# One convolution moved to TensorE, a recurrence cut into two joined segments, and five smaller moves in a hybrid S5 / RWKV-7 layer

## The chip, the cores and the metric

One Trainium2 chip, one of its cores. The metric is the device time of one execution of the whole program in microseconds; three runs of the kernel before gave 1879.26, 1881.02 and 1885.11, and the median, 1881.02, is its time. A separate profiled execution gave the trace that is read below.

## The reference, cut to what matters

A layer over 512 latent tokens with 256 context tokens in front, width 1024, all in fp32. The context goes through the first FFN and the mixers only for the states that it leaves.

```
mod = silu(c) @ w_mod + b_mod            # 9 x 1024, for latents and for context
x   = half_ffn(x);  ctx = half_ffn(ctx)  # SwiGLU, 1024 -> 2816 -> 1024
_, states = token_mixers(modulate(ctx), rows=1, zero states)
out, _    = token_mixers(modulate(x), rows=8, states)
x   = half_ffn(x + mod5 * out);  return rmsnorm(x)

token_mixers(h):  proj = h @ w_in        # u (S5), r k v (RWKV), small ranks, two gates
  S5, both directions, 32 groups x 64 complex states:  s[t] = A s[t-1] + B u[t];  y = C s
  r, k, v = 3x3 depthwise convolution of an image of rows x (n / rows)
  RWKV-7, both directions, 8 heads:  S = S w + (S a) b + v k;  y = S r
  merge: GLU of the S5 output, group norm of the RWKV output, projections, gates, w_out
```

## The kernel before, in words

**Dense work.** Every large product is three matmuls in fp32r, from a high and a low part of the weights and of the activations. A weight block of 128x1024 is loaded from SP's queue (`raw`), rounded by ScalarE (`wh`), and its rest (`wl`) is taken by GpSimd or, where that would be late, by VectorE. The blocks stand in one list, `items`: the context's first FFN, the latents' first FFN with the context's `w_in` blocks between, the latents' `w_in` blocks, then GLU, `w_o`, projection, `w_out` and the second FFN. The generator `dense` works them off in this order.

**What sets the order.** A planner (class `Plan`) runs at build time. Each part is a generator that stops at `yield` with what it needs: tiles, named events, or a pair such as `("P", 3000)`, "GpSimd's planned queue is at most 3000 ns ahead". The planner keeps an estimated clock of each engine, one of the port that GpSimd and VectorE share, and one of the DMA queue, and always runs on the stream of best priority that is ready. So the order of instructions on each engine is fixed when the program is built; on the chip each engine only waits in that order.

**Modulation.** `mod_run` (528) multiplies silu(c) with `w_mod`, in 72 loads of 128 x 4 x 256 (512 KB). 40 of them (shifts, scales and gates 0 to 4) stand at the start, 32 (`fill_run`) beside the latents' first mixer stage. In memory a partition's four rows of 256 lie apart, so each load is in pieces of 1 KB.

**S5.** A chunk is 8 tokens. `s5_build` (957) makes, while the context is worked on, the chunk matrices of 16 pairs of groups for each direction: G (input to state, on GpSimd, X tiles), H (state to output, in `outputs`, on VectorE alone, H tiles), and the impulse response, which goes through memory (Kd, KTd, KTe) into Toeplitz form. It posts `s5b` at its end, after

```
        yield [self.KTd]
        for s in range(8):
            nc.sync.dma_start(self.KTe[s], ...)
        self.sch.post("s5b")
```

`ctx_run` (910) waits for `s5b` before it sets up the context's RWKV stage. `s5_in` fills `hs` with the chunks' inputs, `s5_rec` (1749) runs the recurrence over chunks on GpSimd, four operations of 128 x 64 for each chunk (32 for the context, 64 for the latents):

```
            Pg.tensor_mul(t1, self.arr, h[:, c - 1])
            Pg.tensor_mul(t2, self.aii, h[:, c - 1, ::-1])
            Pg.tensor_add(t1, t1, h[:, c])
            Pg.tensor_add(h[:, c], t1, t2)
```

and `s5_out` (1769) waits for it, then loads H and the Toeplitz blocks and makes the outputs, which `s5_post` turns into the GLU's input. While the latents' recurrence runs, all `wl` go to VectorE.

**RWKV.** First stage (`phase_b1`): `conv_evac` copies a `w_in` block of r, k or v into one of two zero-bordered buffers (10 x 66 for the latents) and scales it with the middle tap; `conv` adds the other eight taps on VectorE. `win_mm` doesn't evacuate block n before convolution n - 2 is done. `v_rows` transposes v on PE, `pa` makes the decays, `pn` the normalised keys, and `pb` (1373) the operands `st`: with tiles `nb`, `kt` and four products on GpSimd, four or five on VectorE, for 4 pairs of heads and two directions. `st` has one buffer, written out by DMA. Second stage (`phase_b2`, for the context in `ctx_run`): `rw_solve` inverts 32x32 triangles for four chunks at a time on VectorE, starting from an identity that GpSimd writes with `affine_select`; `rw_pre` and `rw_main` go through the chunks, 4 for the context and 8 for the latents. In the latents' second stage the gates' `w_in` blocks are run between as filler.

## Time and profile before

| | us |
|---|---|
| median of three runs | 1881.02 (1879.26 to 1885.11) |
| the profiled execution | 1882.93 |
| its span | 1881.2 |
| PE busy | 1681.7 (89%) |
| VectorE (DVE) busy | 1008.5 (54%) |
| ScalarE (ACT) busy | 716.1 (38%) |
| GpSimd (POOL) busy | 655.1 (35%) |

The profiled execution lies 1.7 us above its span and 1.9 us above the median. PE is TensorE's matmuls; the granted clock is given as a share of 2.4 GHz, its other level being 1.2 GHz (0.50). All instructions carry the line of one helper, so groups are told apart by tile names: `wl` is the low part of a weight block, `cvv` the convolved v, `H` and `ms`/`X` the S5 matrices, `t`/`hs` the recurrence, `st` the RWKV operands, `T` and `ti` the solve's result, `yg` the GLU's input. A number such as "x63 | 25.9, 412" is a count, the busy us in all, and the mean ns of one.

### The profile page before, as it was taken

What the parts mean: (1) busy time and instruction counts of PE and PEld (TensorE: products, weight loads), DVE (VectorE), ACT (ScalarE), POOL (GpSimd) and SP (SyncE); (2) the same over time, 40 slices, a digit from 0 to 9 for tenths busy, and PEclk for the clock granted to TensorE, in tenths of its full rate; (3) what the DMA queues carried; (4) which work ended last, traced back from release to release, by engine and by line L of the source; (5) the groups of instructions that cost most, each with busy time, mean ns of one, the idle gap of its engine ahead of it and who ended that gap; (6) DMA issues with size and microseconds to landing.
All of it is one profiled execution on the core that took longest, in us unless ns stands there. A gap on an engine that the chain in (4) does not pass through costs nothing. (4 is left out here: it accounts for less than half of the span.)

```text
span 1881.2 us, 33153 instructions
## 1 busy us (share of the span) xinstructions
PE 1681.7 (89%) x13208; PEld 1409.2 (75%) x13208; DVE 1008.5 (54%) x1763; ACT 716.1 (38%) x1200; POOL 655.1 (35%) x799
## 2 busy tenths in 40 slices
PE   6899999899999989768976879969799999999996
PEld 3699997778887877666544657758689988888886
DVE  3376563755558737444788755644357533333335
ACT  3355442445453213434434323434443342222221
POOL 0134231466664313721334526950015321111111
PEclk9999989899999999887988969979899999999998
DMA  9956551335555464424753484637555223233331
GB/s 308 326 179 193 185 157 58 108 104 148 147 162 150 142 195 154 119 94 130 228 182 101 135 252 150 171 108 199 168 200 181 68 79 101 90 99 102 96 96 56
DMA packets 235626, 278.42 MB, mean 148 GB/s; under 512 B 93617, under 2 KB 186801, under 8 KB 234449
## 3 DMA queue, kind: packets, MB, share of 16 engines
q1 hardware_dynamic: 235472, 276.32, 48.3%
q8 instruction: 104, 1.70, 0.4%
q14 instruction: 50, 0.40, 0.1%
HBM read 234.31 MB, written 43.22 MB: 148 GB/s over the span
## 5 line engine op out<-in xcount | busy, mean ns | idle before, releaser
L209 PE MATMUL b<-hx,wh 128*128 128x512 f32 (+1 forms) x2432 | 704.6, 377 | 19.0 <-ACT wh L209 10.6
L209 POOL TENSOR_TENSOR wl<-raw,wh 128x1024 fp32r<-128x1024 f32 x119 | 292.2, 2457 | 805.7 <-ACT wh L209 748.4
L209 PEld LDWEIGHTS b<-hx,wh 128*128 128x128 f32 x2432 | 444.4, 197 | 103.7 <-issue 16.2
L209 PE MATMUL b<-hx,wl 128*128 128x512 f32 (+1 forms) x1216 | 451.4, 371 | 7.5 <-POOL wl L209 6.5
L209 DVE TENSOR_TENSOR wl<-raw,wh 128x1024 fp32r<-128x1024 f32 x154 | 213.2, 1385 | 291.0 <-ACT wh L209 288.7
L209 ACT CAST wh<-raw 128x1024 fp32r<-128x1024 f32 x273 | 283.1, 1046 | 192.8 <-DMA raw<-in_wgu 67.8
L209 PEld LDWEIGHTS b<-hx,wl 128*128 128x128 f32 x1216 | 238.2, 196 | 48.1 <-POOL wl L209 8.8
L209 PE MATMUL b<-ah,wh 128*128 128x512 f32 (+1 forms) x560 | 196.3, 351 | 0.0
L209 PE MATMUL b<-ah,wl 128*128 128x512 f32 (+1 forms) x560 | 194.4, 347 | 0.3 <-POOL wl L209 0.3
L209 PE MATMUL b<-al,wh 128*128 128x512 f32 (+1 forms) x560 | 194.6, 347 | 0.0
L209 PE MATMUL b<-hc,wh 128*128 128x256 f32 x928 | 174.1, 289 | 1.5 <-ACT hc L209 1.2
L209 PEld LDWEIGHTS b<-hc,wh 128*128 128x128 f32 x928 | 146.5, 193 | 12.6 <-issue 10.0
L209 PE MATMUL b<-hc,wl 128*128 128x256 f32 x464 | 132.0, 284 | 0.0
L209 PEld LDWEIGHTS b<-ah,wl 128*128 128x128 f32 x560 | 107.4, 192 | 13.5 <-POOL wl L209 0.5
L209 PEld LDWEIGHTS b<-ah,wh 128*128 128x128 f32 x560 | 107.3, 192 | 12.7 <-issue 0.2
L209 ACT CAST ah<-prod 128x512 fp32r<-128x512 f32 (+1 forms) x68 | 36.6, 538 | 210.6 <-DVE prod L209 210.6
L209 PEld LDWEIGHTS b<-al,wh 128*128 128x128 f32 x560 | 107.3, 192 | 12.5 <-DVE al L209 0.4
L209 ACT ACTIVATE sil<-b 128x512 f32<-128x512 f32 (+1 forms) x68 | 35.0, 515 | 153.6 <-PE b L209 153.5
L209 DVE TENSOR_TENSOR prod<-sil,b 128x512 f32<-128x512 f32 (+1 forms) x68 | 39.6, 582 | 95.2 <-PE b L209 75.7
L209 PEld LDWEIGHTS b<-hc,wl 128*128 128x128 f32 x464 | 89.6, 193 | 0.0
L209 DVE SCALAR_TENSOR_TENSOR x1c<-b,gp,x1c 128x512 f32<-128x512 f32 (+1 forms) x67 | 43.9, 662 | 74.5 <-PE b L209 74.5
L209 PE MATMUL b<-wmod,zs 128*32 128x256 f32 x576 | 55.7, 478 | 23.4 <-DMA wmod<-in_wmod 23.1
(289 smaller groups left out, 2327.4 us busy)
## 6 DMA issues: line engine op xcount, KB each, us to landing
raw<-in_wgu SPq DMA_DIRECT2D x132, 512.0 KB, 3.8
wmod<-in_wmod SPq DMA_DIRECT2D x72, 512.0 KB, 5.5
raw<-in_wdn SPq DMA_DIRECT2D x66, 512.0 KB, 3.7
raw<-in_win SPq DMA_DIRECT2D x49, 512.0 KB, 3.9
gt<-GTd SPq DMA_DIRECT2D x32, 256.0 KB, 4.0
abk<-st SPq DMA_DIRECT2D x8, 1024.0 KB, 5.8
AB<-abk SPq DMA_DIRECT2D x8, 1024.0 KB, 6.9
GTd<-gst SPq DMA_DIRECT2D x16, 256.0 KB, 2.4
```

The source lines that it names most:

```text
L209: r = f(out, *args, **kw)
```

## The change

1. `w_mod` is laid out in memory so that each load of 512 KB has 4 KB in one piece for a partition.
2. In `s5_build`, VectorE also makes the powers 1 to 16 of the chunk's factor, which are stored (`s5P`). `outputs` takes its work from a list that two streams share: VectorE from the front, GpSimd, when it is through with G, from the back. `s5b` is posted before the KTe copies, and these wait for the end of the context's mixers (`rwc`).
3. For the latents, v is convolved on PE: nine matmuls of a diagonal of the tap's weights (made by GpSimd) with the shifted block, in PSUM. r and k stay on VectorE. The buffers have no border any more; each tap works on the part that it reaches. There are three of them, and block n waits for convolution n - 3.
4. In `pb`, the latents' four GpSimd products go to VectorE. In `pa`, one tile is dropped.
5. `rw_solve`'s identity is two fills by VectorE.
6. The latents' recurrence is cut into two halves of 32 chunks that advance side by side, in operations of 128 x 128; then the second half gets the first's last state times the powers, two chunks at a time. It begins after the event `b2`.
7. `s5_out` asks for its first loads before the recurrence has ended.

```diff
-                nc.sync.dma_start(ws[-1], self.a["wmod"][j, :, k:k + 4, u * 256:(u + 1) * 256])
+                nc.sync.dma_start(ws[-1], self.a["wmod"][j, u, k // 4])
...
+        ps = [half("X").rearrange("p a (k r c) -> p (a k) r c", r=2, c=32) for _ in range(2)]
+        V.tensor_copy(ps[0][:, 0], pw[:, 8])
+        for k, n, o in ((1, 1, (0, 1)), (2, 2, (0, 2)), (4, 4, (0, 4)), (8, 8, (1, 0))):
+            f, d = ps[0], ps[o[0]][:, o[1]:o[1] + n]
+            bc = lambda i: f[:, k - 1, i, None, :].to_broadcast([128, n, 32])
+            cmul(d[:, :, 0], d[:, :, 1], bc(0), bc(1), f[:, 0:n, 0], f[:, 0:n, 1], [t[:, :n] for t in m4], V)
+        for i in range(2):
+            nc.sync.dma_start(self.s5P[:, 8 * i:8 * i + 8], ps[i])
...
+        left = list(range(16))
+
+        def outputs(V, e, names, end):
...
+                if left:
+                    n = left.pop(end)
+                    nxt = [n, *load(n, names[0], a["s5C"])]
...
+                    if o:
+                        V.tensor_scalar(Ct[:, 1], Ct[:, 1], -1.0, None, op0=OP.mult)
...
+        self.sch.add(outputs(V, "V", ("hc", "H", "mh"), 0), S5P)
...
+        yield from outputs(Pg, "P", ("hb", "X", "ms"), -1)
+        yield ["s5hV"]
...
-        yield [self.KTd]
+        self.sch.post("s5b")
+        yield ["rwc", self.KTd]
         for s in range(8):
             nc.sync.dma_start(self.KTe[s], self.KTd[:, :, 7 - s:15 - s].rearrange("i g l o -> i g (l o)"))
-        self.sch.post("s5b")
...
+            w = 2 if r.v else q
+            yield [f"conv{r.s}{n - w}"] * (n >= w) + [f"pb{r.s}{n // q - 2}", f"vr{r.s}{n // q - 2}"] * (n >= 2 * q)
...
+        if r.cvq and not (M_R <= m < M_WD and self.cv_name(m) in ONPE):
+            yield from self.conv_mm(r)
...
+    def taps(self, r, ch):
+
+        self.dg = r.q.tile([128, 9, 128], F32, name="dg")
+        self.nc.gpsimd.affine_select(self.dg, self.cw[:, ch, :, None].to_broadcast([128, 9, 128]),
+                                     pattern=[[0, 9], [1, 128]], base=0, channel_multiplier=-1,
+                                     compare_op=OP.is_equal, fill=0.0)
+
+    def conv_mm(self, r):
...
+        pad, dg = r.pads[n % 3], self.dg
+        yield [pad, dg]
+        px = self.dbank()
...
+        for i, t in enumerate((4, 0, 1, 2, 3, 5, 6, 7, 8)):
+            o, i_ = self.reach(t)
+            self.nc.tensor.matmul(o3[o], dg[:, t], i3[i_], start=i == 0, stop=i == 8, skip_group_check=True)
...
+                B = Pg if r.v else V
...
-                Pg.tensor_mul(nb, fw(nkk, d), ic)
-                Pg.tensor_mul(kt, kt, fw(k, d))
+                B.tensor_mul(nb, fw(nkk, d), ic)
...
-        nc.gpsimd.affine_select(Tt, self.ones[:, 0:32][:, :, None].to_broadcast([128, 32, 32]),
...
+        V.memset(Tt, 0.0)
+        V.memset(Tt.rearrange("p a b -> p (a b)")[:, ::33], 1.0)
...
+        yield [f"s5in{r.s}"] + ["b2"] * (n == 2)
...
+            hc, m = h[:, 1:65].rearrange("p (s c) r k -> p s c r k", s=2), 32
...
+        for c in range(1, m):
+            step((t1, t2, hc[:, :, c]), hc[:, :, c - 1], ar, ai)
             yield [("P", RECP)]
+        for c in (32, 48) if n == 2 else ():
+            Pg.tensor_scalar(sw[:, 0], h[:, c, 1], -1.0, None, op0=OP.mult)
+            Pg.tensor_copy(sw[:, 1], h[:, c, 0])
+            for k in range(0, 16, 2):
...
+                Pg.tensor_mul(t1, p[:, :, 0:1].to_broadcast(w), h[:, c:c + 1].to_broadcast(w))
+                Pg.tensor_mul(t2, p[:, :, 1:2].to_broadcast(w), sw[:, None].to_broadcast(w))
+                Pg.tensor_add(t1, t1, t2)
+                Pg.tensor_add(o, o, t1)
+                yield [("P", RECP)]
...
     def s5_out(self):
...
-        yield ["s5recx"]
+        yield ["s5tab"]
...
         nxt, hts = load_t(0), [load(i) for i in range(HB - 2)]
+        yield ["s5recx"]
```

## Rows read from the trace of the kernel before

**Rows 1.** The page: busy us by engine, and PE's busy tenths by slice.
```profile
PE 1681.7 (89%) x13208; PEld 1409.2 (75%) x13208; DVE 1008.5 (54%) x1763; ACT 716.1 (38%) x1200; POOL 655.1 (35%) x799
...
PE   6899999899999989768976879969799999999996
```
**Rows 2.** Busy time by stretch: stretch, length, engines (instructions), granted clock, DMA share, GB/s.
```profile
0.00:97.00 97.00, 73.66 (x585) 47.81 (x585) 34.75 (x87) 32.88 (x66) 11.82 (x19) 1.00 0.96 318
698.00:806.00 108.00, 84.51 (x1197) 69.87 (x1195) 56.90 (x109) 41.58 (x92) 54.61 (x133) 0.88 0.50 143
877.00:1107.00 230.00, 178.81 (x1394) 120.23 (x1395) 167.44 (x227) 94.22 (x155) 89.39 (x74) 0.83 0.55 168
1230.00:1344.00 114.00, 83.65 (x1956) 74.96 (x1956) 44.32 (x92) 43.14 (x91) 19.64 (x53) 0.88 0.53 151
```
**Rows 3.** PE's waits, 0 to 103 us: for what, total, times, longest.
```profile
PE b L209 <- DMA wmod<-in_wmod: 14.2, 14, 5.0
```
**Rows 4.** DMA issues: count, size of one, median us to landing.
```profile
raw<-in_wgu SPq DMA_DIRECT2D x132, 512.0 KB, 3.8
wmod<-in_wmod SPq DMA_DIRECT2D x72, 512.0 KB, 5.5
```
**Rows 5.** PE's waits, 680 to 806 us.
```profile
PE b L209 <- DVE M L209: 5.8, 1, 5.8
```
**Rows 6.** Timeline of VectorE at two points: start, us, operation.
```profile
582.84 0.43 DVE L209 TENSOR_TENSOR H<-mh 128x256 f32<-128x256 f32 x1
...
662.24 0.42 DVE L209 SCALAR_TENSOR_TENSOR H<-mh 128x256 f32<-128x256 f32 x1
```
**Rows 7.** PE's waits, 877 to 1107 us.
```profile
PE b L209 <- DVE cvv L209: 15.5, 3, 8.0
PE b L209 <- DMA wmod<-in_wmod: 7.6, 6, 3.2
...
PE b L209 <- POOL st L209: 5.0, 2, 3.6
```
**Rows 8.** Groups by shape, 877 to 1107 us: VectorE, then PE.
```profile
L209 DVE SCALAR_TENSOR_TENSOR cvv<-pad,cw,cvv 128x512 f32<-128x512 f32 x32 | 29.8, 930 | 0.8
...
L209 DVE TENSOR_TENSOR st<-nb,em 64x512 f32<-64x512 f32 x8 | 10.4, 1304 | 1.2 <-POOL nb L209 1.2
...
L209 DVE TENSOR_TENSOR st<-cvr,ep 128x512 f32<-128x512 f32 x8 | 6.4, 804 | 0.1
...
L209 PE MATMUL b<-vs,flip 128*128 128x512 f32 x8 | 7.2, 1004 | 1.1 <-ACT vs L209 1.1
L209 PE MATMUL b<-ks,rkb 128*128 128x512 f32 x8 | 5.2, 742 | 0.6 <-DVE ks L209 0.6
```
**Rows 9.** Tile ms: GpSimd's G products, ns least/median/most, first and last start.
```profile
L209 POOL TENSOR_TENSOR ms<-pz,hb x64: 636/650/1636, 349.2 to 542.6; 128x256 f32<-128x256 f32 x64
```
**Rows 10.** Timeline of PE round one rkb product.
```profile
1068.02 1.02 PE L209 MATMUL b<-ks,rkb 128*128 128x512 f32 x2
1068.88 0.49 PE L209 MATMUL b<-ident,rb 128*128 128x128 f32 x3
```
**Rows 11.** Groups by shape on GpSimd, 1107 to 1260 us.
```profile
L209 POOL TENSOR_TENSOR t<-t,hs 128x64 f32<-128x64 f32 x63 | 25.9, 412 | 15.2 <-ACT hs L209 15.2
...
L209 POOL TENSOR_TENSOR hs<-t,t 128x64 f32<-128x64 f32 x63 | 23.5, 374 | 4.9
L209 POOL TENSOR_SCALAR_AFFINE_SELECT Tl<-ones 128x1024 f32<-128x1024 f32 x2 | 3.4, 1678 | 12.9 <-DMA ti<-Tl 12.8
```
**Rows 12.** Timeline of GpSimd: the recurrence's last operation.
```profile
1250.03 0.32 POOL L209 TENSOR_TENSOR hs<-t,t 128x64 f32<-128x64 f32 x1
```
**Rows 13.** Tile Tz: PE's Toeplitz products, ns least/median/most, first and last start.
```profile
L209 PE MATMUL b<-U,Tz x128: 222/222/270, 1275.1 to 1332.3; 128*64 128x64 f32 x128
```
**Rows 14.** PE's waits, 1230 to 1345 us.
```profile
PE b L209 <- ACT yg L209: 7.2, 1, 7.2
```
**Rows 15.** Groups by shape, whole span: GpSimd's G products.
```profile
L209 POOL TENSOR_TENSOR ms<-pz,hb 128x256 f32<-128x256 f32 x64 | 51.0, 816 | 3.3 <-DVE pz L209 1.9
```

151 lines of the change are left out of this document (95 added, 56 removed).

## The prediction

> **What bounds the kernel now.** I read the busy shares first, then the 40 slices, then busy time by stretch, then the waits of the stretches in which TensorE (PE) rests, and at the end single instructions. PE is busy for 1681.7 of 1881.2 us, and most slices read 9 [rows 1]; so the long dense stretches are full, and only PE's idle time, its slow clock and work that is added to PE or taken from it can move the end. The low slices are the first, those round 700 to 800 us, those of 880 to 1110 us, and those round 1240 us. In the table by stretch [rows 2] PE lacks 23.3 us in 0 to 97 us (span less busy time), 23.5 in 698 to 806, 51.2 in 877 to 1107 and 30.4 in 1230 to 1344: 128 of its 199 idle us. The edits lie in or just before these four places, so I price each there.
>
> The profiled execution took 1882.9 us (span 1881.2 and 1.7 around it); the median of the three runs is 1.9 lower. I sum against 1882.9 and take 1.9 off at the end.
>
> **Start (wmod in one piece per partition).** 40 of the 72 wmod loads of 512 KB lie before 97 us; the DMA queues are 0.96 busy there at 318 GB/s [rows 2], and PE waits 14.2 us for wmod, 5.0 of it for the very first load [rows 3]. A weight load of the same size, already in 4 KB pieces, lands in 3.8 us against 5.5 [rows 4]. If that ratio held under full load, the 21 MB of wmod (66 us at 318 GB/s) would shrink by 20 us, more than the waits; if HBM is the limit, by nothing. Of the 9.2 us that are not the first wait I take -6; ends 0 and -14. In the Trainium skill, "DMA: Bandwidth & Descriptors" (Why small descriptors are slow) charges a packet some three cycles beside one for each 32 bytes: 35 cycles for 1 KB, and 131 rather than 140 for 4 KB. By that estimate the 66 us shrink by only 4 us, and the sum would be 2 us less good than mine. The other 32 loads feed the fill in 877 to 1107, where PE waits 7.6 us for them [rows 7]: -2, ends 0 and -5.
>
> **Context: H shared by VectorE and GpSimd, and the KTe copies moved.** GpSimd ends its 16 G groups at 544 [rows 9], when VectorE has finished four of its 16 H groups; the other twelve run from 582.8 to 662.7, 6.6 us each [rows 6, 9]. After the change GpSimd goes on at 544 from the far end. One group costs it four products and two differences of the shape of its G products, 0.65 us each [rows 9], and a small negation: some 4.3 us bare, 6 with the waits that VectorE shows. By 583 it has done six, and the last six split between two engines end near 603, not 663. The new power table costs VectorE about 6 us ahead of G (24 small products at 0.2 to 0.4 us), and the eight KTe copies, with the wait for KTd to land, no longer stand before the event s5b: about 7 us by the eight issues and a landing. So the context's mixer starts some 60 us earlier. What that is worth is PE's idle time in 698 to 806: there the context's recurrence runs with the dense FFN used up, and PE waits longest for masks that VectorE makes behind the solve [rows 5]. Dense work is the same in sum; beside it the chain's holes are filled. Of the 23.5 idle us I take -17, since the last context step and the tail behind it still wait for each other; ends 0 and -30 (all of the idle time and 7 us of its 0.88 clock). The KTe issues come back behind the event rwc, on SP ahead of weight loads; their 6 us stood ahead of weight loads before as well, so I set that move to nothing net, the tail's three loaded blocks hiding it; uncovered it costs up to 6 us.
>
> **Convolution of v on PE, and VectorE for GpSimd's products.** VectorE loses the 32 taps of cvv, 29.8 us [rows 8]. It gains four products for each of eight rounds; VectorE's own of that length cost 1304 ns where GpSimd multiplies beside it, and 804 where it mostly doesn't [rows 8]. At 0.75 us that is 24 us for 32; at 1304 it would be 42. Its old products lose their competitor: about 0.5 us on 24 of them, 12 us, and some 5 on the remaining taps. So VectorE sheds some 23 of its 167 busy us in the stretch, and GpSimd 48 (with four diagonals of 128x1152 added, under 2 us each).
> PE gains nine fp32 matmuls for each of four blocks, on average 464 of 512 columns wide. None stands in the trace; the nearest row is the rkb product, 128x128 by 512 fp32: four of them take 5.2 us, 1.3 each [rows 8]. One of them ran at full clock behind dense work and was left after 0.86 us [rows 10], and the flips, which start cold, take 7.2 us for four, 1.8 each [rows 8]. 36 taps times 464/512 give 28, 42 and 59 us. The taps come behind a dense block, so I take 32. Against it: the stops that PE makes for cvv (15.5 us) and for GpSimd's st (5.0) go [rows 7]; wmod is counted above. That leaves 30.7 of 51.2 idle us. And the granted clock, 0.83 as a mean of its levels of 2.4 and 1.2 GHz [rows 2], rises if PE rests less: the busy 178.8 us are 148 at full clock, so 165 at 0.90. 165 + 32 + 29 = 226 us for a stretch of 230: -4. Ends: +59 (cold taps and no stop removed) and -25 (28 us of taps, 10 idle). VectorE, with 144 of 226 us, doesn't bound it; what is late next is the stop for st (its buffer is written out by DMA).
>
> **Solve's identity.** GpSimd stands 12.8 us before the second one, in the middle of the latents' recurrence [rows 11]. On VectorE the two fills cost under 1 us, but its queue waits for the same write-out; queued behind it are the splits of the next weights, of which two blocks are ahead. I put that at nothing; uncovered it would cost up to 5.
>
> **Recurrence in two segments.** Now 63 steps of four operations on 64 columns: four groups of 63, the largest 25.9 and the smallest 23.5 us [rows 11], 99.8 in all, 0.396 each; the last ends at 1250.4 [rows 12]. After it: 4 at 64 columns, 31 x 4 at 128, and 16 x 4 at 128 to carry the first half into the second, four small ones: 192 rather than 252, but 188 of double width. 128 columns isn't in the trace for GpSimd; the ends are 0.396 and the mean of its 256-column G products, 0.816 [rows 15]. On the line between, 0.54: 188 x 0.54 + 2.6 = 104 us, no shorter than 99.8. What the recurrence gains is the removed stop and the two identities: 12.8 + 2 - 4 = -11 us; ends -37 (0.396: 77 us) and +41 (0.816: 156 us). So I don't count the halved steps as a gain at all.
> The other half of this edit is that Tz, U and the first H are loaded before the recurrence ends. Now the loads are asked for when it has ended, and PE starts the outputs at 1275.1, 25 us after that end [rows 12, 13]. After the change they may start near 1242, into a stretch where PE idles behind the second solve. Eight output groups then fill idle time, rather than lengthening the last RWKV steps; the 7.2 us for yg [rows 14] shrink only partly, since the RWKV chain still ends late. Of the 30.4 idle us I take -12; ends -30 and +16 (recurrence to 1291 and outputs 16 later).
>
> **Sum.** -6 - 2 - 17 - 4 - 12 = -41: 1841.9 in the profiled execution's terms, 1840 against the median.
>
> **Rivals.**
> R1, an earlier context buys nothing: PE is busy 84.5 of 108 us there and the first solve still ends behind the dense work; nor does the second stretch gain, since the second solve (VectorE) and not the recurrence ends last. For it: the longest wait there is for masks that stand behind the solve on VectorE [rows 5]; against it: the lead of 60 us is over half of the stretch. What is left is -6 - 2 - 4 = -12 from 1881: 1869.
> R2, the taps cost what cold fp32 costs: in 877 to 1107 PE works through an order fixed beforehand, and the nine taps, waiting for a copy by ScalarE and a diagonal from GpSimd, start at the low clock as the flips do: +59 there rather than -4, all else as forecast: 1903. It decides from +37 on (then the whole change is even). For it: clock 0.83; against it: a dense block stands right before the taps.
> R3, GpSimd's operation is mostly fixed cost, and 128 columns take the 0.396 of 64: the recurrence ends 37 us earlier, the outputs fill all of the holes (-30), and the context's idle time goes wholly (-30): 1809. Against it: four times the columns take twice the time by these means [rows 11, 15], so columns do count.
> R4, the joined recurrence is longer (0.816): it doesn't do what it says, and ends 41 us later: +16 rather than -12, 1868.
>
> **Numbers.** Forecast 0.46, R1 0.17, R2 0.14, R3 0.15, R4 0.08. The forecast's own range is 1822 to 1858. The range over all is 1800 to 1890: above it lies most of R2 (0.12), below it a part of R3 (0.06). A measurement of this kernel can tell about 0.3%, 5.6 us, from no change. Faster by more: the forecast, R3, most of R1 and half of R4: 0.77. Within: 0.08. Slower by more: R2 and the edges of R1 and R4: 0.15.
>
> **What would show it.** Start: PE's wait for wmod before 97 us under 9 us. Context: the last H near 603, the FFN's dense work still running beside the context's recurrence, no 50 us stretch of small matmuls alone before the FFN's tail. Convolution: no wait for cvv by VectorE, 36 taps of 0.7 to 1.2 us, the stretch from the first w_in block to the last bonus product at 226 us. Recurrence: GpSimd operations of about 0.54 us, 104 us in all. Outputs: first Tz product within 10 us of the recurrence's end. The forecast is wrong if the taps' stretch grows by over 20 us, or if PE is idle for as long as now round 700 to 800 us.

## The result

The changed kernel took 1863.02 us (median of four runs, 1858.08 to 1867.51), the kernel before in the same session 1883.07 (four runs, 1879.26 to 1892.01): a ratio of 0.9886, 95% interval 0.9839 to 0.9933. So -20 us against a forecast of -41. In a second session it took 1870.99 and the kernel before 1886.04, -15 us, a ratio of 0.9923 (0.9896 to 0.9950). The profiled execution took 1867.5 (span 1865.8) and is the slowest of the four.

To see which stretch gave what, I set four landmarks that every kernel here has: one of the last copies of the context's modulation on VectorE, the latents' first small-rank product (`b<-lt,lw`), their last bonus product (`b<-ks,rkb`), and the first `b<-hx,w` product behind the GLU. They cut the span into start, context, convolution, second stage and a tail that ends with PE's last product, some 8 us before the span's end.

| us, from the traces | start | context | convolution | second stage | tail |
|---|---|---|---|---|---|
| before, two executions | 282.0, 280.1 | 601.0, 600.2 | 221.4, 218.6 | 258.8, 258.9 | 509.7, 509.7 |
| after, two executions | 275.8, 277.7 | 597.2, 597.6 | 206.4, 206.7 | 268.8, 266.7 | 509.4, 511.2 |
| forecast | -6 | -17 | -6 | -12 | 0 |
| difference of the means | -4.3 | -3.2 | -13.5 | +8.9 | +0.6 |

Two terms came (start, convolution), one of them at twice its size; two didn't (context, second stage). The spans of these two pairs differ by 11.6 us in the mean, the medians by 20 and 15; what the other executions gain beyond the traced ones isn't in this table. The landmarks also don't cut quite the same work: in the changed kernel 64 of the latents' 256 S5 input products (`b<-U,gt`) have moved from before the last bonus product to behind it. Their records up to that landmark, before and after (tile `gt`; after the length stands PE's busy time):

```profile
877.00:1104.40 227.40, 9.36 (x144) 8.31 (x144) 0.00 (x0) 0.00 (x0) 0.83 0.54 165
```

```profile
867.50:1079.40 211.90, 5.18 (x80) 4.68 (x80) 0.00 (x0) 0.00 (x0) 0.00 (x0) 0.89 0.55 173
```

Some 4 us of the convolution's -13.5 are therefore work that is now counted in the second stage.

The page of the changed kernel, PE's busy time and its slices [rows 1]:

```profile
PE 1696.1 (91%) x13280; PEld 1410.9 (76%) x13280; DVE 994.9 (53%) x1751; ACT 717.5 (38%) x1200; POOL 647.2 (35%) x769
...
PE   7899998899999979978999889968899999999996
```

PE is busy 14.4 us longer, although the kernel is faster. The 17th slice (750 to 800 us) reads 9 where it read 7, but the 15th (650 to 700) has gone from 8 to 7; from 840 to 1120 us 8, 9, 9, 9, 8, 8 stands where 8, 9, 7, 6, 8, 7 stood.

Busy time of the stretches between the same events as in [rows 2] (columns as there):

```profile
0.00:97.00 97.00, 79.20 (x619) 53.83 (x620) 39.00 (x105) 35.01 (x70) 11.81 (x19) 0.96 0.90 328
697.90:797.80 99.90, 93.56 (x1249) 74.30 (x1249) 57.08 (x105) 43.66 (x95) 55.93 (x133) 0.97 0.58 163
867.50:1080.10 212.60, 191.10 (x1401) 122.72 (x1401) 140.90 (x228) 92.35 (x146) 42.81 (x40) 0.89 0.55 173
1200.00:1334.80 134.80, 96.52 (x2115) 86.27 (x2109) 58.26 (x113) 53.34 (x108) 25.93 (x48) 0.81 0.47 126
```

PE's idle time fell from 23.3 to 17.8, from 23.5 to 6.3 and from 51.2 to 21.5 us in the first three, and rose from 30.4 to 38.3 in the fourth. In the second it fell as much as forecast, and yet the context as a whole hardly got shorter: the question of the experiments.

**Start.** PE's waits from 0 to 103 us (for what: us, times, longest), and the DMA issues of the whole span [rows 3, 4]:

```profile
PE b L210 <- DMA wmod<-in_wmod: 7.4, 5, 5.4
```

```profile
wmod<-in_wmod SPq DMA_DIRECT2D x72, 512.0 KB, 4.9
```

What is left is the first load; the landing fell by 0.6 us.

**Context.** PE's two longest waits between 690 and 798 us [rows 5]; VectorE's last H [rows 6]; and GpSimd at the start of its share of H:

```profile
PE b L210 <- DMA gt<-GTd: 5.3, 2, 4.2
PE b L210 <- DVE M L210: 2.6, 3, 1.6
```

```profile
657.93 1.01 DVE L210 TENSOR_TENSOR H<-mh 128x256 f32<-128x256 f32 x1
```

```profile
556.71 0.68 POOL L210 TENSOR_TENSOR st<-kt,em 64x256 f32<-64x256 f32 x1
567.86 1.67 POOL L210 TENSOR_TENSOR ms<-pw,hb 128x256 f32<-128x256 f32 x2 [10.47 <-DMA hb<-in_s5C]
```

The last H is at 658, not at 603: GpSimd began it at 568, not at 544, and first waited 10.5 us for `hb`. From the context's first landmark the last H is no earlier than before (382 us after it, 380 before).

The stretches from 400 to 810 us, before and after:

```profile
400.00:560.00 160.00, 155.75 (x1011) 131.90 (x1011) 91.51 (x167) 79.65 (x136) 107.64 (x111) 1.00 0.52 148
560.00:700.00 140.00, 136.13 (x697) 110.56 (x695) 92.42 (x144) 42.40 (x61) 48.92 (x39) 1.00 0.56 156
700.00:810.00 110.00, 88.27 (x1224) 73.87 (x1225) 59.49 (x111) 43.02 (x94) 55.19 (x133) 0.88 0.48 141
```

```profile
400.00:560.00 160.00, 153.03 (x943) 128.81 (x942) 93.08 (x157) 74.31 (x128) 104.10 (x108) 0.97 0.48 136
560.00:700.00 140.00, 129.34 (x704) 104.49 (x702) 82.07 (x120) 42.98 (x64) 78.70 (x99) 0.97 0.56 154
700.00:810.00 110.00, 103.66 (x1334) 84.79 (x1333) 60.02 (x108) 46.27 (x100) 57.39 (x133) 0.99 0.55 154
```

From 700 to 810 us PE idles 15.4 us less, from 400 to 700 it idles 9.5 us more, and at a lower clock. Busy time times granted clock, an estimate of the work done, rises by 24.9 us in the first and falls by 18.0 in the other.

**Convolution.** Groups by shape, 867 to 1080 us, of PE and VectorE (count | busy us, mean ns | idle before) [rows 8], and PE's waits there [rows 7]:

```profile
L210 PE MATMUL b<-pad,dg 128*128 128x441 f32 x32 | 15.8, 576 | 0.0
...
L210 DVE TENSOR_TENSOR st<-kt,em 64x512 f32<-64x512 f32 x16 | 12.0, 750 | 0.4
...
L210 DVE TENSOR_TENSOR st<-nb,em 64x512 f32<-64x512 f32 x16 | 10.9, 682 | 0.2
...
L210 PE MATMUL b<-vs,flip 128*128 128x512 f32 x8 | 4.2, 605 | 0.9 <-ACT vs L210 0.9
```

```profile
PE b L210 <- DMA gt<-GTd: 9.8, 2, 5.2
...
PE b L210 <- DMA wmod<-in_wmod: 1.5, 3, 0.9
```

All records of tile `dg` in that stretch (busy us of PE, PEld and GpSimd):

```profile
867.50:1080.10 212.60, 33.13 (x72) 13.27 (x72) 7.08 (x4) 0.89 0.55 173
```

The 36 taps are 72 records of `pad,dg`, of four widths. Together they keep PE busy for 33.1 us, 0.92 us for a tap (the records of neighbouring taps overlap, so the busy times of the four widths add up to more), and the group shown has no idle time before it. The stops for cvv (15.5) and for GpSimd's st (5.0) are gone; those for wmod fell from 7.6 to 1.5. The new first wait is for the S5 blocks `gt`.

**Recurrence and outputs.** GpSimd's groups, 1080 to 1240 us [rows 11], tile Tz [rows 13], and PE's longest wait from 1200 to 1335 [rows 14]:

```profile
L210 POOL TENSOR_TENSOR hs<-ys 128x128 f32<-128x128 f32 x31 | 18.3, 590 | 2.4
L210 POOL TENSOR_TENSOR ys<-ys,hs 128x128 f32<-128x128 f32 x31 | 17.6, 567 | 0.0
L210 POOL TENSOR_TENSOR ys<-arr,hs 128x128 f32<-128x128 f32 x31 | 16.5, 531 | 2.4
L210 POOL TENSOR_TENSOR ys<-aii,hs 128x128 f32<-128x128 f32 x31 | 15.9, 514 | 0.0
L210 POOL TENSOR_TENSOR ys<-gt,hs 128x128 f32<-128x128 f32 x16 | 10.2, 635 | 1.1
L210 POOL TENSOR_TENSOR ys<-gt,sw 128x128 f32<-128x128 f32 x16 | 8.9, 558 | 0.0
L210 POOL TENSOR_TENSOR ys<-ys 128x128 f32<-128x128 f32 x16 | 8.4, 526 | 1.3
L210 POOL TENSOR_TENSOR hs<-hs,ys 128x128 f32<-128x128 f32 x16 | 8.0, 499 | 1.3
```

```profile
L210 PE MATMUL b<-U,Tz x128: 222/222/314, 1221.9 to 1309.8; 128*64 128x64 f32 x128
```

```profile
PE b L210 <- DMA T<-ti: 12.3, 2, 11.0
```

The eight groups make 103.8 us for 188 operations, 0.552 each. But the recurrence starts later: 30.8 us after the last bonus product (1079.4) rather than 11.0 (1104.4 before), behind a `wl` block on GpSimd. GpSimd's longest wait from 1079 to 1230 is for that block:

```profile
POOL wl L210 <- ACT wh L210: 18.4, 1, 18.4
```

So it ends 147.8 us after the last bonus product, 146.0 before. The outputs start at 1221.9 rather than at 1275.1; counted from the last bonus product that is 142.5 rather than 170.8 us, 28 us earlier, and the other 25 are the earlier stages'. PE's longest wait there, 11.0 us for T, is for the second solve's result. It was the longest wait before too, from 1230 to 1345 us:

```profile
PE b L209 <- DMA T<-ti: 13.3, 2, 12.1
```

### The profile page after: what moved, and what is told of

Read it like the earlier page. It is cut to its first block, busy times and chain, and to the rows that moved or that the text cites. A ratio compares the mean times of both kernels' runs of the same rounds, so it can differ in the third digit from the quotient of the medians.

```text
span 1865.8 us, 33220 instructions
## 1 busy us (share of the span) xinstructions
PE 1696.1 (91%) x13280; PEld 1410.9 (76%) x13280; DVE 994.9 (53%) x1751; ACT 717.5 (38%) x1200; POOL 647.2 (35%) x769
## 5 line engine op out<-in xcount | busy, mean ns | idle before, releaser
L210 PE MATMUL b<-hx,wh 128*128 128x512 f32 (+1 forms) x2432 | 698.8, 374 | 24.5 <-ACT wh L210 10.5
L210 POOL TENSOR_TENSOR wl<-raw,wh 128x1024 fp32r<-128x1024 f32 x108 | 263.3, 2439 | 810.7 <-ACT wh L210 772.1
L210 PEld LDWEIGHTS b<-hx,wh 128*128 128x128 f32 x2432 | 438.2, 194 | 106.8 <-issue 13.4
L210 DVE TENSOR_TENSOR wl<-raw,wh 128x1024 fp32r<-128x1024 f32 x165 | 227.4, 1379 | 281.9 <-ACT wh L210 271.1
L210 PE MATMUL b<-hc,wh 128*128 128x256 f32 x928 | 178.2, 293 | 1.6 <-ACT hc L210 1.2
L210 DVE TENSOR_TENSOR al<-prod,ah 128x512 fp32r<-128x512 f32 (+1 forms) x68 | 42.7, 628 | 43.0 <-ACT ah L210 43.0
```

What stands on the lines that cost most here:

```text
L210: r = f(out, *args, **kw)
```

## Experiments

There were eighteen further runs, of sixteen new kernels and two repeats. This is the table by landmarks for the new kernels; the ratios are those to the kernel before in the same session, with their 95% intervals. The tails, left out, lie between 506.2 and 513.1 us.

| | start | context | convolution | second stage | median us, ratio |
|---|---|---|---|---|---|
| a1 output loads on GpSimd's queue | 274.9 | 606.1 | 206.0 | 262.0 | 1865.74, 0.9892 (0.9863 to 0.9922) |
| a2 as a1, two output groups early | 274.9 | 600.5 | 205.0 | 262.1 | 1864.51, 0.9884 (0.9854 to 0.9914) |
| a3 one segment | 276.6 | 602.3 | 202.2 | 258.9 | 1862.50, 0.9881 (0.9848 to 0.9913) |
| a4 v on VectorE | 276.6 | 602.3 | 222.2 | 261.9 | 1882.84, 0.9985 (0.9958 to 1.0011) |
| b1 pb ahead of H on GpSimd | 277.6 | 618.8 | 210.9 | 264.3 | 1881.50, 0.9983 (0.9960 to 1.0007) |
| b2 H on VectorE alone | 276.5 | 612.0 | 209.9 | 264.2 | 1884.83, 1.0016 (0.9991 to 1.0042) |
| b3 b1 and a3 | 276.0 | 611.6 | 201.7 | 261.2 | 1878.34, 0.9937 (0.9906 to 0.9967) |
| c2 a3 and a1 | 275.8 | 599.5 | 206.1 | 266.9 | 1867.58, 0.9893 (0.9866 to 0.9921) |
| c3 no recurrence of the latents | 279.9 | 597.0 | 210.3 | 258.1 | 1861.84, one run |
| c4 products on GpSimd | 277.2 | 600.9 | 200.5 | 262.6 | 1862.07, 0.9870 (0.9839 to 0.9901) |
| d1 start and convolution | 278.7 | 612.9 | 203.4 | 264.1 | 1884.23, 0.9992 (0.9970 to 1.0013) |
| d2 d1 and context | 278.4 | 602.1 | 205.1 | 259.1 | 1858.45, 0.9862 (0.9836 to 0.9887) |
| d3 a3 and c4 | 277.6 | 601.0 | 205.9 | 261.1 | 1863.25, 0.9879 (0.9852 to 0.9906) |
| e1 d1 in the context's old order | 278.0 | 599.5 | 208.7 | 258.0 | 1863.57, 0.9869 (0.9839 to 0.9898) |
| e2 start and context | 280.5 | 599.9 | 228.6 | 259.6 | 1885.42, 0.9989 (0.9972 to 1.0007) |
| e3 d2 in that way | 276.6 | 594.3 | 204.9 | 264.9 | 1862.52, 0.9873 (0.9842 to 0.9904) |

The two repeats are b4, the kernel before (1877.6, one run), and c1, the changed kernel; their landmarks stand in the first table.

### What the convolution is worth

**a4** puts v back on VectorE and leaves all else as changed:

```diff
-ONPE = "v"
+ONPE = ""
```

> The changed kernel with the convolution of v back on VectorE (all else of the change stays: pads without a border, the other products on VectorE, wmod in one piece). Theory T: taking 32 taps from VectorE is what shortened the stretch from the first w_in block to the last bonus product (228 to 213 us): VectorE gets some 25 us back and PE waits for the convolution again, the stretch returns to 222 to 230 and the run is 8 to 15 us longer. Rival: the stretch was shortened by the shorter taps, by the wmod loads and by products that no longer compete with GpSimd: under 5 us longer.

Measured: 222.2 us in the convolution, and no measurable difference to the kernel before. **c4** is the changed kernel with the bonus round's products back on GpSimd:

```diff
-                B = Pg if r.v else V
+                B = Pg
```

> The changed kernel with the four products of each bonus round back on GpSimd, v still on PE. VectorE sheds 32 products of about 0.7 us (23 us) in the stretch of the convolution, and its other products and taps lose some of their speed beside GpSimd. Theory V (VectorE bounds the convolution): the stretch gets shorter or stays, 198 to 207 us. Theory P (the shared work is what stretched VectorE before): VectorE's remaining taps and products take 0.9 to 1.3 us each again, PE waits for st as before (5 us), and the stretch is 3 to 8 us longer than the changed kernel's 202 to 211.

Measured: 200.5 us, 6 less than the changed kernel. The stretch between the two landmarks, in a4 and in c4 (columns as in [rows 2]):

```profile
878.90:1101.10 222.20, 174.64 (x1398) 116.43 (x1396) 160.86 (x256) 94.34 (x155) 42.91 (x38) 0.81 0.54 170
```

```profile
878.10:1078.60 200.50, 182.66 (x1406) 118.57 (x1404) 144.63 (x199) 91.31 (x147) 80.67 (x67) 0.92 0.58 184
```

With v on VectorE, PE is idle for 47.6 us at a clock of 0.81; with v on PE for 17.8 at 0.92. Its busy time grows by only 8.0 us, although the taps are added, since the other products run at the higher clock. GpSimd's 80.7 busy us in c4 stop nobody. So the convolution's place is the gain; the products' move to VectorE, which was half of that edit, brought nothing. Over all kernels with v on PE this stretch has a mean of 206.5 us with the products on VectorE (10 executions) and 204.8 with them on GpSimd (6); with v on VectorE it is 222.7 (4). The moved S5 products don't explain this: in d1 and e3 144 of them stand before the last bonus product, as in the kernel before, and the stretch has 203.4 and 204.9 us.

### What the context edit is worth

**b1** makes GpSimd's H groups give way to the context's bonus round `pb`, which stands behind them in the changed kernel; **b3** is the same with one segment; **b2** takes GpSimd's share of H away:

```diff
-                yield [Ct, (e, S5V if e == "V" else S5Q)]
+                yield [Ct, (e, S5V)]
...
-                    yield [(e, S5V if e == "V" else S5Q)]
+                    yield [(e, S5V)]
```

```diff
-        yield from outputs(Pg, "P", ("hb", "X", "ms"), -1)
```

> The changed kernel, where GpSimd's H products are queued only when GpSimd is 0.6 us from idle by the planner's clock, not 3 us as now; so the context's bonus products (nb, kt, st) slip in between them. Theory Q (queue): the context's mixer starts no earlier after the change because the last three rounds of these products stand behind GpSimd's ten H groups (before: kt at 559, 577 and 588 us; after: 643, 658 and 668). Then they run again before 610, the last lf write is issued before 620 instead of at 686, the first solve begins 10 to 20 us earlier (now 696 to 700) and the stretch up to the latents' first lora product (873 to 881) shrinks by 5 to 15 us. Rival E (an earlier context buys nothing): the first solve begins earlier, the end of the stretch stays within 4 us. Rival H: VectorE's last H group (658) binds all the same, and the solve begins within 4 us of now.

> The changed kernel with the recurrence in one segment and the bonus products let in between the H products (the two edits of two other runs together). If they add up: the stretch from the last bonus product of the latents to the first w_o product at 259 us (the changed kernel 262 to 269), VectorE's two solves at 46 us busy instead of 55, the first solve of the context 10 to 20 us earlier; in all 8 to 20 us under the changed kernel. If an earlier context buys nothing: 0 to 8 us under it.

> The changed kernel with all sixteen H groups on VectorE again, none on GpSimd; the KTe copies stay behind the mixer's start. Theory Q: the bonus products run at 560 to 590 us again, the last H near 660, and the first solve begins within 4 us of the changed kernel's 696 to 700: the share of GpSimd was worth nothing. If the share was worth what the prediction said, H ends 30 us or more later than in the changed kernel and the run is 8 to 17 us longer.

Measured: with pb first, its last write goes out at 624 us rather than at 686, but the last H comes at 672 on VectorE and at 677 on GpSimd, and the context takes 618.8 us (b3: 611.6). With H on VectorE alone the last H comes at 695 and the first solve starts at 732, 36 us later than in the changed kernel; the context grows by only 15. So whatever GpSimd does second is late, and a start of the solve that is 36 us off moves the end by less than half of that. The expectations are missed: b1's first solve starts at 710.7, later rather than earlier, and b2 is 14 to 22 us slower than the changed kernel, which by its expectation would mean that GpSimd's share is worth what was forecast. But the order of the context's instructions changes in all three, so they can't tell the share from the order; d1 to e3 can.

**d1** keeps of the whole change only the start and the convolution (the functions `s5_build`, `s5_rec`, `s5_out`, `rw_solve` and GpSimd's products are those of before); **d2** puts the context edit back:

> Only the start (wmod in one piece) and the convolution of v on TensorE are kept; the kernel before's H on VectorE alone, its KTe copies ahead of s5b, its one-segment recurrence, its late output loads, its identity by GpSimd, and the bonus round's products on GpSimd. Theory N (the context, recurrence and output edits are worth nothing or cost): last modulation copy to the first small-rank product of the latents 600 us, as before and after; from there to the last bonus product 200 to 206; from there to the first hx,w product 259; span 1855 to 1860, at or below that of the changed kernel. Theory G (those edits gain what they were meant to, and something else in the change eats it): span above the changed kernel's 1863 to 1870, with the context 5 us or more longer than 600.

> The run without context, recurrence and output edits, and the context edit put back (H shared by VectorE and GpSimd, power table, KTe copies behind rwc). Theory N: within 4 us of that run, context 598 to 602 us. Theory G: 5 us or more faster than it in the context (595 or less).

Measured: d1 gains nothing (0.9992), d2 25 us (0.9862). Both went against the theory that the context edit is idle: by these two it is worth everything. But d1's context is 12 us longer than that of before, which has the same code for S5. The order of its instructions differs, from the context's first decays on; of the edits left in d1, the tile dropped in `pa` alone brings such a difference at the same place. **e1** is d1 with `pa` as before for the context, **e3** is d2 with it, and **e2** is the kernel before with the start and context edits:

```diff
+                if r.v:
+                    cm = q.tile([128, nch, 65], F32, name="cm")
+                    V.tensor_sub(cm, s65, s65[:, :, 32:33].to_broadcast([128, nch, 65]))
+                    yield [cm, ("A", 1000)]
...
+                if r.v:
+                    A_.activation(ep, cm, AF.Exp, scale=-KAPPA)
+                    A_.activation(em, cm, AF.Exp, scale=KAPPA)
```

> As d1 (start and convolution alone), but the small edit in pa (the dropped tile) only for the latents: for the context it is as before. With that the order of instructions on TensorE, VectorE and GpSimd is that of the kernel before up to the latents' convolutions; in d1 it wasn't, from the context's first decays on. Theory O (the 12 us that d1 lost in the context are the price of the changed order, which the dropped tile brings; the context edit only pays that back): last modulation copy to the first small-rank product of the latents 600 to 602 us (d1: 612.9), then 203 to 206, then 259 to 264, span 1858 to 1866, ratio 0.988 to 0.991: the gain of the whole change without the context edit. Theory G (the context stretch is long because H and s5b are late, and the context edit repairs that): the stretch stays at 608 or more, ratio 0.995 to 1.

> The kernel before with the start edit and the context edit alone (H shared, power table, KTe copies behind rwc; no convolution on TensorE, no dropped tile, the recurrence and outputs as before). Theory O: context 598 to 603 us, the rest as before, ratio 0.997 to 0.999 (the start's 4.5 us at most). Theory G: context 590 or less, ratio 0.992 or less.

> d2 (start, convolution, context) with the dropped tile only for the latents. If the dropped tile's order costs 12 us in itself, and the context edit is worth 12 in itself, the context takes 588 to 592 and the span is 1848 to 1852. Theory O: 598 to 603 as in d2, span 1855 to 1863, since both orders with the context edit end at the same wait: the S5 products behind H.

Measured: e1, without any context edit, has 599.5 us in the context and a ratio of 0.9869: the gain of the whole change. e2, with it, has 599.9 and 0.9989. d1 and e1 differ in nothing but that tile. The stretch from 400 to 560 us in d1:

```profile
400.00:560.00 160.00, 141.90 (x845) 119.06 (x846) 85.28 (x171) 67.38 (x117) 99.80 (x108) 0.89 0.44 127
```

The same in e1:

```profile
400.00:560.00 160.00, 155.47 (x1037) 131.49 (x1036) 92.18 (x167) 81.24 (x140) 107.45 (x113) 1.00 0.51 148
```

In this stretch of d1 PE executes 845 rather than 1037 matmuls, is idle for 18.1 rather than 4.5 us, and the clock is 0.89. The idle time is made up later: over the whole context (first d1, then e1) it is 60.1 and 61.0 us.

```profile
sum 612.90, PE 552.80 PEld 459.92 DVE 330.86 ACT 240.39 POOL 278.76; mean PE 110.56 PEld 91.98 DVE 66.17 ACT 48.08 POOL 55.75
```

```profile
sum 599.50, PE 538.47 PEld 451.11 DVE 343.20 ACT 240.01 POOL 271.07; mean PE 107.69 PEld 90.22 DVE 68.64 ACT 48.00 POOL 54.21
```

By busy time times granted clock PE does the same work in both, some 510 us at full clock (an estimate, summed over five stretches). So the 13 us between the two traces are work done at the lower clock: 552.8 busy us against 538.5. (By the ratios d1 is some 23 us slower than e1; d1's profiled execution is one of the two fastest of its twelve, and what the others lose beyond these 13 isn't in a trace.) The context edit changes the order in the same place, so with the dropped tile it takes 11 of those us back (d2), and without it there is little for it to take: e3 is at 594.3, and its ratio of 0.9873 is e1's. The expectation's 588 to 592 for two independent gains is missed.

Where the earlier start goes is seen in e1 and e3, whose first solves start at 709.1 and 689.2 us. First e1, then e3:

```profile
560.00:700.00 140.00, 131.05 (x644) 106.47 (x643) 90.96 (x141) 38.32 (x54) 46.53 (x35) 1.00 0.55 150
700.00:810.00 110.00, 91.09 (x1248) 76.61 (x1249) 59.75 (x112) 43.16 (x94) 55.68 (x133) 0.88 0.49 140
```

```profile
400.00:560.00 160.00, 154.34 (x979) 130.20 (x978) 85.45 (x156) 76.27 (x134) 103.50 (x106) 0.97 0.50 140
560.00:700.00 140.00, 129.79 (x708) 104.80 (x707) 83.72 (x127) 40.97 (x65) 81.00 (x104) 0.95 0.57 154
700.00:810.00 110.00, 104.63 (x1322) 87.53 (x1321) 63.00 (x106) 48.06 (x99) 55.81 (x133) 1.00 0.53 149
```

Busy time by granted clock: from 700 to 810 us e3 does 104.6 us of full-clock work, e1 80.2, a gain of 24. From 400 to 700 it does 273.0 against 286.5, a loss of 13.5: less dense work is done in that stretch, and the clock drops there. That the context's small products have come forward and push it out is my reading; between 700 and 810 us e3 has more matmuls than e1 (1322 against 1248). What remains at the end of the context is 5 us, in this pair only; over 13 executions with H shared and pb behind it the context has a mean of 600.1 us, against 600.2 in the three with the order of before.

### What the recurrence and the outputs are worth

**a3** makes the latents' recurrence one segment again and drops its power table:

```diff
-        Pg, h, n = self.nc.gpsimd, r.hs, 1 if r.v else 2
+        Pg, h, n = self.nc.gpsimd, r.hs, 1
...
-            hc, m = h[:, 1:65].rearrange("p (s c) r k -> p s c r k", s=2), 32
+            hc, m = h[:, 1:65].rearrange("p (s c) r k -> p s c r k", s=1), 64
```

> The changed kernel with the latents' recurrence in one segment of 63 steps and no power table; the early loads of Tz, U and the first H stay. GpSimd's operations should be 252 of about 0.40 us, 100 us against 104. Theory of the prediction (the two segments gain nothing by themselves): total within 4 us of the changed kernel, the recurrence's end within 5 us of 1227. Rival (the halved number of steps is the gain): the recurrence ends 20 us or more later and the run is 8 us or more longer.

Measured: 258.9 us in the second stage, that of before, and 1862.50 us. The recurrence ends at 1224, as expected, but the outputs stand late again in PE's order: their first product comes 171.5 us after the last bonus product, as before (170.8) and not as in the changed kernel (142.5). So a3 undoes the early outputs too. **c3** leaves the latents' recurrence out altogether; its outputs are released by the event `pre8`, behind the first RWKV step of the second solve:

```diff
             Pg.tensor_copy(h[:, 0], self.s5e)
+            yield ["pre8"]
+            self.rec = False
+            self.sch.post("s5recx")
+            return
```

> Left out: the latents' S5 recurrence itself, so the states enter the outputs without it; the outputs are released behind the first RWKV step of the second solve, as with one segment. Theory C (contention): VectorE's two solves take 42 to 45 us for the same 124 operations with GpSimd quiet (one segment 46.3, two segments 55.2), and each solve ends 5 us or more earlier than in the changed kernel. Rival: the solves stay near 55 us busy, then it was not GpSimd's recurrence that stretched them. It also shows what any faster recurrence could give at most: the time from the last bonus product to the first w_o product against 259 to 269.

Measured: 258.1 us. A kernel with no recurrence at all is no faster there than the kernel before. T comes 3.2 us earlier than before, counted from the last bonus product (151.8 against 155.0), but the outputs, held until `pre8`, start at 167.7 and end at 229.6 (230.6 before), and PE's last long wait is for yg, 7.9 us (7.2 before). So a shorter recurrence by itself gains nothing as long as the outputs keep this place in PE's order; what early outputs would give beside undisturbed solves, no run shows.

In the seven executions whose outputs start early (142 to 144 us after the last bonus product: the changed kernel twice, a1, a2, a4, b1, b2) it is the RWKV chain that ends last: from T to its last product it takes 93.9 us in the changed kernel, 65.1 before, and the GLU stands right behind it on PE. These stretches, before and after:

```profile
1259.50:1324.60 65.10, 59.42 (x1473) 53.58 (x1473) 22.05 (x36) 27.00 (x60) 0.00 (x0) 0.94 0.69 194
```

```profile
1241.00:1334.90 93.90, 74.25 (x1581) 66.69 (x1580) 28.97 (x55) 39.74 (x82) 1.27 (x1) 0.81 0.54 143
```

Of the 28.8 us, 14.0 are idle time of PE and most of the rest is its lower clock; the one output group more that stands in the chain, seven rather than six, takes some 3.2. And T itself comes later, 161.5 rather than 155.0 us after the last bonus product. That is the wider recurrence's doing: it disturbs VectorE's solves. VectorE's 62 products of the two solves (tile prod: ns least/median/most), in the changed kernel, in a3 and in c3:

```profile
L210 DVE TENSOR_TENSOR prod<-Tl,AT x62: 181/424/658, 1098.2 to 1233.8; 128x31 f32<-128x31 f32 x4, 128x60 f32<-128x60 f32 x4, 128x87 f32<-128x87 f32 x4, 128x112 f32<-128x112 f32 x4
```

```profile
L210 DVE TENSOR_TENSOR prod<-Tl,AT x62: 180/375/528, 1101.7 to 1230.1; 128x31 f32<-128x31 f32 x4, 128x60 f32<-128x60 f32 x4, 128x87 f32<-128x87 f32 x4, 128x112 f32<-128x112 f32 x4
```

```profile
L210 DVE TENSOR_TENSOR prod<-Tl,AT x62: 182/359/2531, 1104.8 to 1225.9; 128x31 f32<-128x31 f32 x4, 128x60 f32<-128x60 f32 x4, 128x87 f32<-128x87 f32 x4, 128x112 f32<-128x112 f32 x4
```

The median is 424 ns beside GpSimd operations of 128 columns, 375 beside those of 64, 359 with an idle GpSimd. All 124 operations of the two solves take 55.2, 46.3 and 44.6 us. Over all traces they take 55.0 to 56.0 us beside 128 columns (8 executions) and 44.5 to 46.6 beside 64 (11), so the width matters clearly, and 64 columns against none only by the medians of single traces. The Trainium skill, "SBUF — State Buffer" (Who interferes with whom), says that a VectorE instruction with two inputs in SBUF contends with a GpSimd one that reads SBUF, over a shared pair of ports that it calls an exclusive lock. The traces agree in direction; the 65 ns added here are far less than a whole GpSimd operation of 552.

**a1** moves the output stage's H loads and y writes from SP's queue to GpSimd's, **a2** also holds the second RWKV chain back until two output groups are done, and **c2** is a1 with one segment:

```diff
-            nc.sync.dma_start(H.rearrange("p d r f -> p (d r f)"), ...)
+            nc.gpsimd.dma_start(H.rearrange("p d r f -> p (d r f)"), ...)
...
-            yield [M, t1]
+            yield [M, t1] + ["out2"] * (p == 8)
```

> The changed kernel, with the output groups' H loads and yd writes issued on GpSimd's DMA queue instead of SP's; PE's order is the same. Theory W (waits): what the earlier outputs gained is lost because these DMAs and the T loads of the RWKV chain stand in each other's way on SP (ScalarE stands 8.3 us before ys for yd<-ys, and PE waits for Z behind it): then that stall goes, the second and third chain steps after the second solve (now 21 and 27 us) fall to about 16, and the run is 8 to 11 us shorter than the changed kernel. Theory L (in line): each output group of 3.2 us now stands between the chain's own products and lengthens it, whichever queue loads it: then the chain from the second solve's T to the yg products stays at 90 to 94 us and the run gains under 4 us.

> As the run before (H loads and yd writes on GpSimd's queue), and the second output group is put in PE's order ahead of the chain's product that waits 11 us for the second solve's T. Theory L: a second group of 3.2 us goes into the idle hole and out of the chain, so the run is 3 us shorter than the run before. Theory W: the hole still holds the H load's latency, the group ends at the same time as T lands, and the gain over the run before is 0 to 2 us.

> The changed kernel with the recurrence in one segment, and the outputs' H loads and yd writes on GpSimd's queue. If the 128-column operations on GpSimd slow VectorE's solves (55 us busy against 46 with 64 columns) and the SP queue costs the chain behind the second solve some 5 us, both add up: 252 to 257 us from the last bonus product to the first w_o product (one segment alone 258.9, the queue alone 262), the run 6 to 12 us shorter than the changed kernel beside it. If the outputs are late again because the recurrence is no shorter, the queue finds nothing to shorten: 259, and 3 to 8 us shorter.

Measured: 262.0, 262.1 and 266.9 us. The first looks like 5 to 7 us against the changed kernel, but c2, which should have added a3's gain to it, is as long as the changed kernel. A second output group in the hole brings nothing over the first. The queue isn't shown to matter; neither theory of a1 came as told (the chain from T to yg took 84.0 us, T came 3 us later, and the run gained nothing). Even the stage's unchanged code gave 258.0 to 264.9 in seven executions of six kernels (before twice, d1, d2, e1, e2, e3: mean 260.5); two segments gave 261.9 to 268.8 in eight (mean 264.1), one segment in the changed order 258.9 to 266.9 in four (a3, b3, c2, d3: mean 262.0). Some 4 us is what the edit of recurrence and outputs costs by these means, with the early outputs in seven of the eight; the changed kernel's +8.9 also holds the S5 products that moved behind the landmark, and a share of order that I can't separate.

**d3** puts the two partial reversals together, a3 and c4:

> The changed kernel with one segment in the recurrence and the bonus round's products on GpSimd: both parts that earlier runs showed to be of no use are undone. If the gains add up: 202 us to the last bonus product and 259 from there to the first hx,w product, with the context at 600: span 1853 to 1857, 6 to 10 us below the changed kernel. If the two are not independent (GpSimd's products delay the recurrence, and with it the outputs): 202 and 263 or more, span 1860.

Measured: 205.9 and 261.1 us, 1863.25. Neither part keeps its single price: the gains don't add up. Two repeats show what an execution alone moves:

> The kernel before once more, for the spread of the places in its trace: the context's last normalised block at 282 us, the first lora product of the latents at 883, 221 us from there to the last bonus product, 259 from there to the first w_o product. If executions differ by as much as the five profiles of the changed order do (873 to 881 us for the first lora product), this one lies between 879 and 887.

> The changed kernel once more, for its spread and beside the other three of this call: solves of VectorE 55 us busy, 202 to 211 us from the first lora product of the latents to the last bonus product, 262 to 269 from there to the first w_o product, context from its last normalised block to the first lora product 597 to 606 us. Median within 6 us of 1863.

Measured: each landmark interval agrees with the first execution's within 3 us. The changed kernel's median, 1870.99, is 2 us outside the expected 6.

No version stands out from the better ones: a3, c4, d2, d3, e1 and e3 lie between 0.986 and 0.988, with intervals that overlap. d2 has the lowest median, 1858.45.

## Why the prediction was wrong, point by point

- **Start, -6: right in kind, too large.** All 18 executions with the new layout have a mean of 277.2 us at the first landmark, against 281.1: -3.9. The rate rose only from 318 to 328 GB/s. The estimate from the packet cost in the Trainium skill, "DMA: Bandwidth & Descriptors" (Why small descriptors are slow), weighed in the prediction, was -4 where I took -6; the traces agree with it.
- **Context, -17: this step failed, and it is the first reason for the miss.** It was put as "So the context's mixer starts some 60 us earlier. What that is worth is PE's idle time in 698 to 806". The mixer's first solve starts 13.6 us earlier (709.9 to 696.3), 6.2 of them by the start in this pair: GpSimd began H 24 us late (G, which began 11 us later behind the power table and the blocks that the planner put there, ended at 556, and then GpSimd waited for `hb`), and the last rounds of pb, which stood before H, now stand behind it. I counted GpSimd's H as an addition to an idle engine and not as something that its other work queues behind. The second half of the step is the more general error: PE's idle time in that stretch did go (23.5 to 6.3), but its dense work had come from the stretch ahead, where PE idles 9.5 us more and runs slower. e1 without the context edit and e3 with it have the same ratio (0.9869 and 0.9873). R1 had this outcome, with a chance of 0.17, but for another reason, a first solve that stays behind the dense work. The sign that the prediction named for this step, as much idle time as before round 700 to 800 us, didn't come: it looks at the hole alone and not at the stretch ahead.
- **Convolution, -4, and the later wmod loads, -2: right in sign, too small.** -13.5 between the landmarks of the pairs, -16.8 by the means over all kernels (222.7 to 205.9). The stretch of 230 us has become 212.6 rather than 226. The taps took 33 us (32 forecast) and the clock is 0.89 (0.90), but PE is busy 191.1 rather than 197 us and idle 21.5 rather than 29. The mis-sized terms are the idle time, of which I let only the named stops go, and the busy time of the old work, 158 rather than 165 us: 4.2 us of it are the S5 products that left the stretch, and some of the rest ran faster untouched, as the flips, which went from 7.2 to 4.2 us now that PE doesn't stop for cvv. The sum also took the 2 us of wmod twice, since the 29 idle us (30.7 less 2) hold them already. Cold taps (R2) didn't come.
- **The products on VectorE** took 0.68 to 0.75 us, as forecast. c4 shows that they needn't have moved.
- **Solve's identity, nothing: not refuted.** VectorE waits 4.9 us for the write-out of the first solve's tile, less than GpSimd's 12.8. No run changes this edit alone.
- **Recurrence: right in size**, 188 operations at 0.552 us, 103.8 in all (0.54 and 104 forecast). R3 and R4, which lived from other sizes, are out. Its end was to come 11 us earlier; it takes 18 us less from start to end (135.0 to 117.0), but a start 20 us later, which the prediction didn't consider, takes that back.
- **Outputs, -12: this step failed too, +9 in the pair, +4 by means.** The first product comes 28 us earlier from the last bonus product (33 forecast), but only one output group fits before the second solve's result. That result is 6.5 us late because VectorE's chain of small operations is slowed by the wider GpSimd ones, a cost that the forecast put at nothing, and the RWKV chain behind it takes 29 us longer. I read the stretch's idle time as waiting for the recurrence. The row that the prediction went by, [rows 14], shows 7.2 us for ScalarE's yg at the end; the longest wait of the stretch, 13.3 of its 30.4 idle us, was for the second solve's T, as R1 has it in its second half. c3 shows that the stretch is as long with no recurrence and the outputs in their old place.

With the context and the outputs at nothing the forecast's own sum is -12, R1's 1869. By the means of the landmarks it is -4 for the start, nothing for the context, -17 for the convolution and +4 for the second stage: -17, where the two sessions' medians gave -20 and -15.

## What to carry to other kernels

Idle time of the bounding engine beside a dependent chain is a gain only if the chain ends earlier and the dense work that fills the hole isn't taken from a stretch that was already full, so add up the work over both. Before an engine off the path is made faster, leave its work out in one run, and look at the longest wait of the stretch: c3 shows that a shorter recurrence could not gain while the outputs keep their place, and PE's 13.3 us for T stood in the trace of before. Where a planner writes the order, a change of one small tile can move a stage by more than the edit under test (12 us here); fix the order for what isn't tested, or compare stages over many kernels, before an edit is credited or blamed.

## What was not expected of the hardware

- An fp32 product of 128x128 by some 464 columns, issued behind dense work, takes 0.92 us on PE (33.1 us for 36) at a granted clock of 0.89; nine of them with shifted views replace 29.8/4 = 7.5 us of eight VectorE operations by 8.3 us.
- Small VectorE operations with two inputs (31 to 256 columns) slow down beside wide GpSimd operations: medians of 359, 375 and 424 ns at none, 64 and 128 columns, and 44.5 to 46.6 against 55.0 to 56.0 us for 124 of them beside 64 and 128.
- GpSimd's two-input operation on 128 partitions took 0.396 us for 64 columns, 0.552 for 128 and 0.816 for 256 (means; the median of the last is 0.650 [rows 9]): by the line through the first two, an estimate, 0.24 us of it is fixed.
